# Moving seven of twelve modulation rows from TensorE, between attention units, to VectorE row sums

## The chip, the cores and the metric

The kernel runs on one core of one Trainium2 chip. The metric is the device time of one execution in microseconds (us). Five engines work side by side, each through a queue of its own in the order in which the program was built: TensorE (PE, with its weight loads as PEld), VectorE (DVE), ScalarE (ACT), GpSimd (POOL) and SyncE (SP), which issues the loads from memory. An instruction that waits holds up everything behind it on its engine.

## What is computed

Two transformer blocks follow each other. The first has two layers over 512 tokens (256 of a context, 256 of the sequence), and its normalised activations are shifted, scaled and gated by vectors that come from a condition:

```python
def adaln(cond, w_mod, b_mod):
    m = jnp.dot(jax.nn.silu(cond), w_mod) + b_mod
    return jnp.split(m[..., None, :], 6, axis=-1)

def modulate(h, shift, scale):
    return h * (1.0 + scale) + shift
```

`w_mod` is 1024 x 6144 for each layer, and there are two conditions (`c` for the sequence, `c_ctx` for the context), so a layer has six modulation rows ("which" 0 to 5: shift, scale and gate of the attention half, then of the feed-forward half) of 1024 numbers, for each condition. A layer is then: modulated norm, projections to q, k, v, a pooling branch and a convolution branch, four attention heads, an output projection gated by row 2, a modulated norm with rows 3 and 4, and a feed-forward of 1024 to 2816 to 1024 gated by row 5. In the second layer only the sequence's half of the tokens is carried past the keys and values, so that rows 2 to 5 are needed there for one condition. The second block (four branches, one layer) is untouched by the change.

## The kernel before

Activations lie with features on the 128 partitions and tokens along the free axis: `xT` is 128 x 8 x 512. Every large product is made of three fp32r products (high by high, low by high, high by low). `weights` (line 328) loads a 512 KB chunk of packed weights into `wraw` (4 buffers), ScalarE rounds it to `whi` (L333) and VectorE subtracts to get `wlo` (L334), each with 3 buffers; `mm3` (line 342) issues the three matmuls (L343 to L345). `feats` (line 359) makes one feature tile of 8 x 3 matmuls from one chunk, `tok` (line 387) makes token tiles.

`modulation` (line 491) is a generator that makes one group, one modulation row of one layer (1024 columns). In each of 8 steps a 512 KB chunk of `w_mod` comes into `wmod` (2 buffers), and four matmuls with 32 stationary columns (L497) add to the PSUM bank `ps_md`, of which there is one. After the eighth step ScalarE copies the bank (L502), TensorE transposes it twice (L504), and VectorE adds the bias (L517). Each of the four matmuls stands as two records in the trace, so that a step is 8 records.

`fill` (line 534) takes the next steps from `queue`, which holds groups 2 to 5 of layer 0 and all six of layer 1 (line 854). It is called at fixed places with the counts of `FILL` (line 28), n times four steps each: behind the transposes of each head's q and k (lines 893, 897 and 904), before the output projection (line 929), and behind the last product of the output projection and of the feed-forward (lines 941 and 984). The instructions get a lower priority than their neighbours. The order on each engine is then made by the Tile scheduler, which takes, of what is ready, the highest priority, and whose order is fixed when the program is built.

`attention` (line 636) goes over 16 units in layer 0 (4 heads x 4 token tiles) and 8 in layer 1. A unit's chain is: scores on TensorE, row maximum on VectorE (L651), exponential on ScalarE (L653), the weighted difference on VectorE (L662), transposes (L665), a copy on ScalarE (L667), the product with v (L670), the square on ScalarE (L674) and a scaled copy on VectorE (L675). `each` (line 875) runs after every unit. `project_rows` (line 818) makes the output projection in 16 steps of 12 matmuls (8 feature tiles in two parts), each closed by two VectorE additions into `xT` (L797). `norm` (line 467) makes the next `h` in two halves of 8 tiles (L479 on VectorE, or L476 and L477 on GpSimd, then L481 on ScalarE and L482 on VectorE). The feed-forward (from line 944) goes in three thirds of 8, 7 and 7 hidden tiles; a hidden tile is two `feats`, and a third ends with 8 projection steps.

Of the kernel before, what the change touches and what calls it, by code (L numbers as in the profile page):

```python
# [21 lines left out]
KD = D // 128  # L22
# [4 lines left out]

FILL = ((2, 2, 3, 3, 2, 1, 1), (2, 2, 2, 0, 0, 2, 9))
LATE = 60
AHEAD = (2, 0)  # L30
POOL_AFTER = ((14, 15), (5, 6))
# [5 lines left out]

MOD_GROUPS = {0: ((4, 5, 0, 1), (6, 7, 2, 3)) + tuple(tuple(range(4 * i, 4 * i + 4)) for i in (4, 2, 3, 5)),
              1: tuple(tuple(range(4 * i, 4 * i + 4)) for i in (1, 0, 4, 2, 3, 5))}

# [11 lines left out]
def _weight_plan():  # L52
# [3 lines left out]
    def rows(key, name, lead, cols, r0, kt):  # L56
        plan[key] = (name, lead, r0, np.asarray(cols), kt)

    qk_cols = (np.arange(8)[:, None] * 64 + HALVES[None, :]).ravel()
    for l in range(DEPTH):  # L60
        for g, parts in enumerate(MOD_GROUPS[l]):
            cols = np.concatenate([np.arange(c * 256, c * 256 + 256) for c in parts])
            for k in range(8):
                rows(("mod", l, g, k), "w_mod", (l,), cols, k * 128, 1)
        if l == 0:
# [51 lines left out]
def _pack_weights(inp):  # L117
    out = np.zeros((len(PLAN), 128, CHUNK), np.float32)
    for key, (name, lead, r0, cols, kt) in PLAN.items():
        a = np.asarray(inp[name])[lead]  # L120
        a = a[r0:r0 + kt * 128] if isinstance(r0, int) else np.concatenate([a[k * 128:k * 128 + 128] for k in r0])
# [49 lines left out]
def _rows():  # L171
    at, off = {}, 0
    for name, n in (("qkg", 256), ("subg", 256), ("qna", 64), ("kna", 64), ("qnc", 64), ("knc", 64), ("lnv", 512),
                    ("bf", 8)):
        at[name] = (off, n)
        off += n
    return at, off
# [5 lines left out]
def _pack_rows(inp):  # L183
    src = dict(qkg=np.stack([np.asarray(inp[n])[:, HALVES] for n in ("q_norm_g", "k_norm_g")]),
               subg=inp["subln_g"], qna=inp["qn_a_2"], kna=inp["kn_a_2"], qnc=inp["qn_c_2"],
               knc=inp["kn_c_2"], lnv=inp["ln_v_g_2"], bf=inp["b_forget_2"])
    return np.concatenate([np.asarray(src[k]).reshape(1, -1) for k in ROWS], axis=1)
# [78 lines left out]
def tile_two_blocks(ctx: ExitStack, tc: tile.TileContext, w: bass.AP, blk: bass.AP, cols: bass.AP,  # L266
# [30 lines left out]
    def open_consts(second):  # L297
        c0, c1 = (CST1, NCST) if second else (CST0, CST1)
        r0, r1 = (ROW1, NROWS) if second else (0, ROW1)
        ct = P["cst"].tile([128, c1 - c0], F32, name="cstt")  # L300
# [49 lines left out]
    def bank(p):  # L350
        return P[p].tile([128, 512], F32, name="ps_" + p)
# [181 lines left out]

    def fill(n, late=LATE):

        at = tc.cur_priority
        tc.cur_priority = at + late
        for _ in range(n * KD // 2):
            while queue and next(queue[0], None) is None:
                queue.pop(0)  # L540
        tc.cur_priority = at


# [303 lines left out]
    for l in range(DEPTH):  # L847
# [5 lines left out]
        if not last:  # L853
            queue.extend([modulation(0, g) for g in range(2, 6)] + [modulation(1, g) for g in range(6)])
        mix = {}
# [12 lines left out]
        def run_taps(m):  # L868
            for _ in range(min(m, len(taps))):
                taps.pop(0)()  # L870
# [4 lines left out]
        def each():  # L875
            run_taps(8)
            unit[0] += 1
            if jobs and unit[0] in POOL_AFTER[l]:
                jobs.pop(0)()
# [5 lines left out]
        for hd in range(0, 4, 2 if last else 1):  # L885
# [3 lines left out]
            if last:  # L889
                tok([("k", l, g, i) for i in range(2)], h, range(4),  # L890
                    lambda tt, p: rope(l, slice(1, 2), tt, kq[tt][:, 0:256], p))
                kT = to_feature(kq, 0, range(4))
                fill(FILL[l][hd])
                tok([("q", l, g, i) for i in range(2)], h, qts,
                    lambda tt, p: rope(l, slice(0, 1), tt, kq[tt][:, 256:512], p))
                qT = to_feature(kq, 256, qts)
                fill(FILL[l][hd + 1])
            else:
# [4 lines left out]
                kT = to_feature(kq, c + 128, range(4), 1)  # L903
                fill(FILL[l][hd])
            if hd == 0:
# [22 lines left out]
        conv_norm(l, acc, seqs, mix)  # L928
        fill(FILL[l][4])
        project_rows(l, range(KD), lambda d: merge(0, d), range(4), 2, False, 0, lo, None)  # L930
# [8 lines left out]
        project_rows(l, range(KD), lambda d: merge(1, d), range(4), 2, True, 0, lo, after)  # L939
        with tc.issue_after(P["product"].ins):  # L940
            fill(FILL[l][5], -50)

        for t, (f0, f1) in enumerate(THIRDS):
            hs = []
            f = f0
            items = []
            for f in range(f0, f1):
# [16 lines left out]
                for it in items:  # L964
                    feats([it], h, [(lo, 512)])
                items = []
            final = t == 2
            if final:
# [3 lines left out]
                def after2(d, a, b):  # L972
# [633 lines left out]
```

## Time and profile before

| what | value |
|---|---|
| time, median of 3 runs | 1467.88 us (1460.85, 1467.88, 1469.97) |
| the profiled execution's own time | 1452.94 us |
| its span in the trace | 1451.1 us |
| mean granted TensorE clock | 0.98 |
| busy PE, DVE, ACT, POOL | 1385.5, 854.4, 619.0, 233.3 us |

The span runs from the first to the last instruction of the profiled execution. Times below are microseconds from its start. A busy PE is pipelined matmuls, so that its busy time says when it had work, not how dense that was. In the span, the first norm ends at about 65, the attention of layer 0 runs from about 178 to 239, its output projection from 239 to 286.6, the norm behind it to 311, the three thirds of the first feed-forward from 311 to 655, the next norm and the start of layer 1 from 655, and the q, k and v of layer 1 to about 766.

### The profile page before, as it was taken

The page shows a single profiled execution, that of the slowest core. Times are in us where ns is not written, and L with a number is a line of the kernel's source. Part 1 is how long each engine was busy: PE and PEld are TensorE (multiplying, and loading weights), DVE is VectorE, ACT ScalarE, POOL GpSimd, SP SyncE. Part 2 cuts the span into 40 slices and gives each one's busy share as a digit, 9 for nine tenths or more (in the row PEclk, how much of TensorE's full clock was granted, in tenths as well). Part 3 has the DMA queues.
Part 4 walks back from the last instruction along what each step waited for, and adds up shares of the span by engine and source line. Part 5 has one row for each costly group of instructions (what it writes and reads, how often), then busy time and mean ns, then how long its engine had stood idle before and what let it go on. Part 6 is the DMA issues. An engine that isn't in the chain of part 4 may idle for free. (4 is left out here: it accounts for less than half of the span.)

```text
span 1451.1 us, 23265 instructions
## 1 busy us (share of the span) xinstructions
PE 1385.5 (95%) x9212; PEld 1191.6 (82%) x9212; DVE 854.4 (59%) x1592; ACT 619.0 (43%) x1100; POOL 233.3 (16%) x274
## 2 busy tenths in 40 slices
PE   5999999999999999999998899999989997999999
PEld 2787766888888888888867889999977887988999
DVE  4688665653333343338966655565786665657555
ACT  3333444342222222235344544444645549456443
POOL 0045440220000000013515210000452002000000
PEclk9999999999999999999999989999999999999999
DMA  8635654333322233225562335555743422434553
GB/s 332 238 117 195 204 196 146 103 115 102 97 91 102 86 104 102 90 85 189 198 227 71 106 127 187 176 189 174 240 148 113 148 77 78 146 113 149 189 178 128
DMA packets 60733, 212.49 MB, mean 146 GB/s; under 512 B 6864, under 2 KB 8016, under 8 KB 60368
## 3 DMA queue, kind: packets, MB, share of 16 engines
q1 hardware_dynamic: 60192, 208.85, 43.0%
q10 hardware_dynamic: 432, 2.16, 0.4%
q8 instruction: 72, 1.18, 0.3%
q14 instruction: 37, 0.30, 0.1%
HBM read 209.93 MB, written 1.05 MB: 145 GB/s over the span
## 5 line engine op out<-in xcount | busy, mean ns | idle before, releaser
L333 ACT CAST whi<-wraw 128x1024 fp32r<-128x1024 f32 (+2 forms) x296 | 304.8, 1033 | 536.2 <-PE ps_mm L344 268.8
L334 DVE TENSOR_TENSOR wlo<-wraw,whi 128x1024 fp32r<-128x1024 f32 (+2 forms) x296 | 359.6, 1217 | 229.1 <-ACT whi L333 225.7
L343 PE MATMUL ps_mm<-hH,whi 128*128 128x256 f32 (+1 forms) x1056 | 344.4, 328 | 7.7 <-ACT hH L481 7.0
L345 PE MATMUL ps_mm<-hH,wlo 128*128 128x256 f32 (+1 forms) x1056 | 342.7, 326 | 2.7 <-DVE wlo L334 2.7
L344 PE MATMUL ps_mm<-hL,whi 128*128 128x256 f32 (+1 forms) x1056 | 343.3, 326 | 0.3 <-DVE hL L482 0.3
L343 PEld LDWEIGHTS ps_mm<-hH,whi 128*128 128x128 f32 x1056 | 203.7, 194 | 29.0 <-ACT hH L481 9.3
L345 PEld LDWEIGHTS ps_mm<-hH,wlo 128*128 128x128 f32 x1056 | 204.4, 194 | 19.7 <-DVE wlo L334 3.3
L344 PEld LDWEIGHTS ps_mm<-hL,whi 128*128 128x128 f32 x1056 | 204.2, 194 | 19.6 <-issue 2.7
L343 PE MATMUL ps_mm<-hidH,whi 128*128 128x256 f32 (+1 forms) x683 | 214.9, 317 | 3.0 <-ACT hidH L339 1.7
L344 PE MATMUL ps_mm<-hidL,whi 128*128 128x256 f32 (+1 forms) x683 | 214.4, 315 | 0.6 <-DVE hidL L340 0.6
L345 PE MATMUL ps_mm<-hidH,wlo 128*128 128x256 f32 (+1 forms) x683 | 213.7, 314 | 0.0
L344 PE MATMUL ps_mm<-wlo,hH 128*128 128x256 f32 (+2 forms) x464 | 145.2, 314 | 3.3 <-DVE wlo L334 3.3
L343 PE MATMUL ps_mm<-whi,hH 128*128 128x256 f32 (+2 forms) x464 | 143.0, 317 | 0.6 <-ACT whi L333 0.6
L345 PE MATMUL ps_mm<-whi,hL 128*128 128x256 f32 (+2 forms) x464 | 143.2, 310 | 0.0
L343 PEld LDWEIGHTS ps_mm<-hidH,whi 128*128 128x128 f32 x683 | 129.2, 190 | 12.3 <-ACT hidH L339 1.9
L344 PEld LDWEIGHTS ps_mm<-hidL,whi 128*128 128x128 f32 x683 | 129.4, 189 | 9.2 <-DVE hidL L340 0.9
L345 PEld LDWEIGHTS ps_mm<-hidH,wlo 128*128 128x128 f32 x683 | 129.1, 190 | 8.1
L454 POOL TENSOR_TENSOR squares<-squares,scr 128x256 f32<-128x256 f32 (+1 forms) x28 | 30.2, 1077 | 562.3 <-ACT scr L453 561.9
L797 DVE SCALAR_TENSOR_TENSOR xT<-ps_mm,modv,xT 128x256 f32<-128x256 f32 x116 | 52.6, 479 | 99.0 <-PE ps_mm L345 98.8
L348 POOL TENSOR_TENSOR st<-st,mhalf 128x4 f32<-128x4 f32 (+3 forms) x54 | 67.3, 1251 | 214.7 <-DVE st L581 100.0
L344 PEld LDWEIGHTS ps_mm<-wlo,hH 128*128 128x128 f32 x464 | 88.5, 191 | 14.1 <-DVE wlo L334 6.1
L343 PEld LDWEIGHTS ps_mm<-whi,hH 128*128 128x128 f32 x464 | 87.3, 190 | 13.7 <-issue 8.3
(339 smaller groups left out, 1940.4 us busy)
## 6 DMA issues: line engine op xcount, KB each, us to landing
wraw<-in_w_dram SPq DMA_DIRECT2D x271, 512.0 KB, 3.5
wmod<-in_w_dram SPq DMA_DIRECT2D x85, 512.0 KB, 4.2
wraw<-in_w_dram SPq DMA_DIRECT2D x32, 448.0 KB, 3.2
xT<-in_x_dram ACTq DMA_DIRECT2D x2, 1024.0 KB, 6.9
single<-in_w_dram SPq DMA_DIRECT2D x8, 256.0 KB, 7.2
wraw<-in_w_dram SPq DMA_DIRECT2D x4, 288.0 KB, 2.8
out_dram<-scr SPq DMA_DIRECT2D x8, 128.0 KB, 1.7
tm<-in_blk_dram SPq DMA_DIRECT2D x3, 256.0 KB, 4.4
```

The lines of the kernel that those rows point to most:

```text
L333: act.copy(out=hi[:, :m], in_=t[:, :m])
L334: dve.tensor_tensor(lo[:, :m], t[:, :m], hi[:, :m].bitcast(F32), op=ALU.subtract)
L343: pe.matmul(ps, a[0], b[0], start=start, stop=False)
L344: pe.matmul(ps, a[0], b[1], start=False, stop=False)
L345: P["product"] = pe.matmul(ps, a[1], b[0], start=False, stop=stop)
L348: pool.tensor_tensor(t, t, mhalf[:, :n], op=ALU.pow)
L454: eng.tensor_tensor(squares[:, lo:hi], squares[:, lo:hi], q, op=ALU.add)
L797: dve.scalar_tensor_tensor(xT[:, d, r], ps[:, s * 256 - lo:s * 256 - lo + 256], M(l, which, 1 - s)[:, d:d + 1], xT[:, d, r], op0=ALU.mult, ...
```

## The change

Of the ten groups that went through `fill`, three stay (layer 0, rows 2, 4 and 3). They now run two steps after each of the first 12 attention units of layer 0. The other seven (layer 0 row 5, and all six of layer 1) are made by VectorE in a new generator, called three steps per hidden tile in the first feed-forward's code. For these `w_mod` is packed transposed, so that a chunk holds 128 output columns on the partitions and the 1024 inputs along the free axis; each half row of 512 is multiplied by the silu of the condition, spread over the partitions, and summed by one instruction into one column of `sums`. There are 8 chunks per row; a chunk takes 4 such sums where both conditions are needed (three rows) and 2 where one is (four rows). The product itself goes to the PSUM bank `ps_md` and is not read.

```diff
-FILL = ((2, 2, 3, 3, 2, 1, 1), (2, 2, 2, 0, 0, 2, 9))
+FILL = (2,) * 12
+BY_ROWS = ((0, 5), (1, 1), (1, 0), (1, 2), (1, 4), (1, 3), (1, 5))
+ROWS_PER_STEP = 3
...
+    def modulation_by_rows():
+
+        crow = [P["tm"].tile([128, 512], F32, name="tm") for _ in range(4)]
+        o = ROWS["cc"][0]
+        for i, t in enumerate(crow):
+            dma.dma_start(out=t, in_=rowv[:, o + i * 512:o + i * 512 + 512].broadcast_to([128, 512]))
+            act.activation(t, t, AF.Silu)
+        for l, which in BY_ROWS:
+            js = range(2 if l == 0 or which < 2 else 1)
+            sums = {j: st(16) for j in js}
+            for d in range(KD):
+                t = raw_chunk(("modr", l, which, d), "wmod")[0]
+                for j in js:
+                    for i in range(2):
+                        dve.tensor_tensor_reduce(bank("md"), t[:, i * 512:i * 512 + 512], crow[2 * j + i], 1.0, 0.0,
+                                                 ALU.mult, ALU.add, sums[j][:, i * KD + d:i * KD + d + 1])
+                if d < KD - 1:
+                    yield
...
-            queue.extend([modulation(0, g) for g in range(2, 6)] + [modulation(1, g) for g in range(6)])
+            queue.extend(modulation(0, g) for g in range(2, 5))
...
         def each():
             run_taps(8)
+            if not last and unit[0] < len(FILL):
+                fill(FILL[unit[0]])
...
-                fill(FILL[l][hd])
...
-        fill(FILL[l][4])
...
-        with tc.issue_after(P["product"].ins):
-            fill(FILL[l][5], -50)
-
+        rows = modulation_by_rows() if not last else None
...
+                if not last:
+                    for _ in range(ROWS_PER_STEP):
+                        next(rows, None)
...
-        with tc.issue_after(P["product"].ins):
-            fill(FILL[l][6], -50)
```

Where the seven rows land is decided by the scheduler. The first place is VectorE's queue in the output projection of layer 0 (`xT` is the addition that closes a step, `wlo` the low half of a weight chunk, `hidL` the low half of an attention output). Before:

```order
L797 SCALAR_TENSOR_TENSOR xT<-ps_mm,modv_112,xT 128x256 x4
L334 TENSOR_TENSOR wlo<-wraw,whi 128x1024
L340 TENSOR_TENSOR hidL<-ps_aux,hidH 128x512
L340 TENSOR_TENSOR hidL<-cacc,hidH 128x512 x2
L797 SCALAR_TENSOR_TENSOR xT<-ps_mm,modv_112,xT 128x256 x4
L334 TENSOR_TENSOR wlo<-wraw,whi 128x1024
L797 SCALAR_TENSOR_TENSOR xT<-ps_mm,modv_112,xT 128x256 x4
```

And in the changed kernel, where `ISA ps_md` is a sum and `ISA st` the read of its accumulator:

```order
L567 ISA ps_md,st_3321<-wmod,tm 128x512
L567 ISA st_3321 128x1
L835 SCALAR_TENSOR_TENSOR xT<-ps_mm,modv_112,xT 128x256 x2
L567 ISA ps_md,st_3320<-wmod,tm 128x512
L567 ISA st_3320 128x1
L344 TENSOR_TENSOR wlo<-wraw,whi 128x1024
L835 SCALAR_TENSOR_TENSOR xT<-ps_mm,modv_112,xT 128x256 x2
L567 ISA ps_md,st_3320<-wmod,tm 128x512
L567 ISA st_3320 128x1
L835 SCALAR_TENSOR_TENSOR xT<-ps_mm,modv_112,xT 128x256 x2
```

The sums have moved up: counted over the whole queue, 64 of the 160 stand ahead of the first norm behind the attention (from the tenth unit on), 19 inside that norm, and 77 in the first third of the feed-forward; none stands behind it.

The second place is ScalarE's queue in the attention of layer 0, where `e` is the exponential and `tm` at L559 the silu of the spread condition. In the changed kernel:

```order
L559 ACT_TABLE_LOAD
L559 ACTIVATE tm<-tm 128x512
L712 ACTIVATE sq_1720,st_1674<-ps_aux,st_1707 128x128
L705 COPY aT<-ps_aux 128x256
L559 ACTIVATE tm<-tm 128x512
L691 ACT_TABLE_LOAD
L691 ACTIVATE e,st_1906<-ps_sc,st_1905 128x256
L559 ACT_TABLE_LOAD
L559 ACTIVATE tm<-tm 128x512
L691 ACT_TABLE_LOAD
L691 ACTIVATE e,st_1906<-ps_sc,st_1905 128x256
L559 ACT_TABLE_LOAD
```

In the kernel before there is one table load ahead of the first exponential of that attention and none between its units. A piece of its queue there, with the same square, copy and exponential:

```order
L674 ACTIVATE sq_1940,st_1894<-ps_aux,st_1927 128x128
L667 COPY aT<-ps_aux 128x256
L653 ACTIVATE e,st_2070<-ps_sc,st_2069 128x256
L674 ACTIVATE sq_1980,st_1894<-ps_aux,st_1967 128x128
L653 ACTIVATE e,st_2070<-ps_sc,st_2069 128x256
L667 COPY aT<-ps_aux 128x512
```

So four silus and six table loads now stand between the exponentials, three changes to the silu table and three back.

The third place is TensorE's queue at the start of layer 1, where `tm` is transposed for keys and queries. Before:

```order
L497 MATMUL ps_md<-wmod,csil 32x256
L620 MATMUL ps_aux<-first,tm 128x128 x2
L497 MATMUL ps_md<-wmod,csil 32x256 x3
L343 MATMUL ps_mm<-whi,hH 128x256
L344 MATMUL ps_mm<-wlo,hH 128x256
L345 MATMUL ps_mm<-whi,hL 128x256
```

And in the changed kernel:

```order
L658 MATMUL ps_aux<-first,tm 128x128 x2
L355 MATMUL ps_mm<-whi,hL 128x256
L353 MATMUL ps_mm<-whi,hH 128x256
L354 MATMUL ps_mm<-wlo,hH 128x256
L355 MATMUL ps_mm<-whi,hL 128x256
L353 MATMUL ps_mm<-whi,hH 128x256
```

The modulation's matmuls are gone there, and the projections stand directly behind the transposes.

## Rows read from the trace of the kernel before

**Rows 1.** The page's first part: busy time, share and instructions by engine

```profile
PE 1385.5 (95%) x9212; PEld 1191.6 (82%) x9212; DVE 854.4 (59%) x1592; ACT 619.0 (43%) x1100; POOL 233.3 (16%) x274
```

**Rows 2.** Stretches: start:end, length, busy by engine (instructions), clock, DMA share, GB/s

```profile
core 0: us, PE busy (x) PEld busy (x) DVE busy (x) ACT busy (x) POOL busy (x), PEclk, DMA share, GB/s
65.00:178.00 113.00, 113.00 (x885) 91.74 (x885) 90.40 (x171) 41.99 (x101) 49.69 (x55) 1.00 0.50 169
178.00:202.80 24.80, 23.68 (x164) 15.45 (x161) 17.41 (x38) 11.31 (x34) 16.60 (x31) 1.00 0.62 213
202.80:239.00 36.20, 31.93 (x236) 19.73 (x236) 22.75 (x60) 19.23 (x54) 6.43 (x8) 0.95 0.62 203
239.00:286.60 47.60, 47.60 (x261) 41.25 (x259) 27.17 (x53) 16.41 (x26) 8.97 (x8) 1.00 0.21 69
286.60:311.00 24.40, 21.36 (x175) 19.20 (x174) 15.97 (x33) 10.64 (x23) 10.65 (x11) 0.93 0.37 127
311.00:446.00 135.00, 135.00 (x605) 112.09 (x605) 51.34 (x61) 37.63 (x46) 0.00 (x0) 1.00 0.31 102
655.00:690.00 35.00, 33.67 (x251) 28.17 (x251) 29.22 (x63) 18.45 (x33) 12.54 (x11) 0.90 0.56 196
690.00:766.00 76.00, 74.17 (x625) 58.79 (x623) 57.94 (x125) 31.85 (x73) 31.44 (x32) 1.00 0.61 208
```

**Rows 3.** The same stretches, the modulation's matmuls (L497) alone: PE, PEld, clock, DMA

```profile
65.00:178.00 113.00, 20.37 (x182) 5.51 (x182) 1.00 0.50 169
202.80:239.00 36.20, 8.31 (x104) 2.04 (x104) 0.95 0.62 203
286.60:311.00 24.40, 2.38 (x32) 0.77 (x32) 0.93 0.37 127
655.00:690.00 35.00, 5.71 (x52) 1.57 (x52) 0.90 0.56 196
690.00:766.00 76.00, 14.43 (x172) 4.00 (x172) 1.00 0.61 208
```

**Rows 4.** Groups by line: the modulation's matmuls and transposes; busy, mean ns, idle before

```profile
L497 PE MATMUL ps_md<-wmod,csil 128*32 128x256 f32 x640 | 59.7, 393 | 9.8 <-DMA wmod<-in_w_dram 9.7
...
L504 PE MATMUL ps_md<-first,cp 128*128 128x128 f32 x20 | 4.2, 295 | 0.0
```

**Rows 5.** Groups by line and form: VectorE instructions over 512 elements; busy, mean ns

```profile
L340 DVE TENSOR_TENSOR hidL<-scr,hidH 128x512 fp32r<-128x512 f32 x24 | 16.3, 684 | 0.0
L662 DVE SCALAR_TENSOR_TENSOR e<-e,st 128x512 f32<-128x512 f32 x16 | 13.4, 839 | 0.5
```

**Rows 6.** Timeline of VectorE: multiply-and-reduce of the second block; start, length

```profile
1281.08 0.42 DVE L1346 CUSTOM_DVE_ANT_0 e<-ps_sc,cstt 128x256 f32<-128x256 f32 x1
...
1281.43 0.29 DVE L1346 CUSTOM_DVE_ANT_0 e<-ps_sc,cstt 128x128 f32<-128x128 f32 x1
...
1281.64 0.42 DVE L1346 CUSTOM_DVE_ANT_0 e<-ps_sc,cstt 128x256 f32<-128x256 f32 x1
```

**Rows 7.** Groups by line: ScalarE's table load, and an activation over 512 elements

```profile
L653 ACT ACT_TABLE_LOAD x2 | 2.6, 1283 | 0.0
...
L952 ACT ACTIVATE scr<-ps_mm 128x512 f32<-128x512 f32 x21 | 12.4, 589 | 0.0
```

**Rows 8.** Timeline of VectorE in the first feed-forward: two weight chunks

```profile
330.33 1.23 DVE L334 TENSOR_TENSOR wlo<-wraw,whi 128x1024 fp32r<-128x1024 f32 x1
...
335.76 1.22 DVE L334 TENSOR_TENSOR wlo<-wraw,whi 128x1024 fp32r<-128x1024 f32 x1 [3.61 <-ACT whi L333]
```

**Rows 9.** Loads of wmod: from issue to landing

```profile
DMA to landing us min/median/max: 3.3/4.2/10.3
```

**Rows 10.** Timelines of VectorE and GpSimd: pairs of convolution taps, one beside GpSimd

```profile
82.20 1.40 DVE L769 SCALAR_TENSOR_TENSOR cacc<-cu,colt,cacc 128x512 f32<-128x512 f32 x2
...
87.78 1.87 DVE L769 SCALAR_TENSOR_TENSOR cacc<-cu,colt,cacc 128x512 f32<-128x512 f32 x2
...
87.92 1.19 POOL L607 TENSOR_TENSOR tm<-tm,own 128x256 f32<-128x256 f32 x1
```

More of the change, by code (lines that the diff above doesn't have):

```diff
@@ L34 @@
 NXS = 3
-MOD_GROUPS = {0: ((4, 5, 0, 1), (6, 7, 2, 3)) + tuple(tuple(range(4 * i, 4 * i + 4)) for i in (4, 2, 3, 5)),
-              1: tuple(tuple(range(4 * i, 4 * i + 4)) for i in (1, 0, 4, 2, 3, 5))}
+MOD_GROUPS = {0: ((4, 5, 0, 1), (6, 7, 2, 3)) + tuple(tuple(range(4 * i, 4 * i + 4)) for i in (2, 4, 3))}
 MIX_PARTS = ((0, 1, 4, 5), (6, 7, 2, 3))
@@ L60, in _weight_plan @@
     for l in range(DEPTH):
-        for g, parts in enumerate(MOD_GROUPS[l]):
+        for g, parts in enumerate(MOD_GROUPS.get(l, ())):
             cols = np.concatenate([np.arange(c * 256, c * 256 + 256) for c in parts])
@@ L64, in _weight_plan @@
                 rows(("mod", l, g, k), "w_mod", (l,), cols, k * 128, 1)
+        for which in range(6):
+            if (l, which) in BY_ROWS:
+                for d in range(8):
+                    plan[("modr", l, which, d)] = ("w_mod", (l,), ("T", which * D + d * 128), np.arange(D), 1)
         if l == 0:
@@ L120, in _pack_weights @@
         a = np.asarray(inp[name])[lead]
+        if not isinstance(r0, int) and r0[0] == "T":
+            out[INDEX[key]] = a[:, r0[1]:r0[1] + 128].T
+            continue
         a = a[r0:r0 + kt * 128] if isinstance(r0, int) else np.concatenate([a[k * 128:k * 128 + 128] for k in r0])
@@ L173, in _rows @@
     for name, n in (("qkg", 256), ("subg", 256), ("qna", 64), ("kna", 64), ("qnc", 64), ("knc", 64), ("lnv", 512),
-                    ("bf", 8)):
+                    ("bf", 8), ("cc", 2048)):
         at[name] = (off, n)
@@ L185, in _pack_rows @@
                subg=inp["subln_g"], qna=inp["qn_a_2"], kna=inp["kn_a_2"], qnc=inp["qn_c_2"],
-               knc=inp["kn_c_2"], lnv=inp["ln_v_g_2"], bf=inp["b_forget_2"])
+               knc=inp["kn_c_2"], lnv=inp["ln_v_g_2"], bf=inp["b_forget_2"],
+               cc=np.stack([np.asarray(inp["c"])[0], np.asarray(inp["c_ctx"])]))
     return np.concatenate([np.asarray(src[k]).reshape(1, -1) for k in ROWS], axis=1)
@@ L298, in open_consts @@
         c0, c1 = (CST1, NCST) if second else (CST0, CST1)
-        r0, r1 = (ROW1, NROWS) if second else (0, ROW1)
+        r0, r1 = (ROW1, ROWS["cc"][0]) if second else (0, ROW1)
         ct = P["cst"].tile([128, c1 - c0], F32, name="cstt")
@@ L532, in tile_two_blocks, with fill @@
     queue = []
-    def fill(n, late=LATE):
+    def fill(n):
         at = tc.cur_priority
-        tc.cur_priority = at + late
-        for _ in range(n * KD // 2):
+        tc.cur_priority = at + LATE
+        for _ in range(n):
             while queue and next(queue[0], None) is None:
@@ L541, in fill @@
         tc.cur_priority = at
+    def modulation_by_rows():
[15 more added lines that the diff above has]
+                    yield
+            bias = C(f"bmod{l}")[:, which * 8:which * 8 + 8]
+            for j in js:
+                m = M(l, which, j)
+                dve.tensor_tensor(m, sums[j][:, :KD], bias, op=ALU.add)
+                dve.tensor_tensor(m, m, sums[j][:, KD:], op=ALU.add)
+                if which in (1, 4):
+                    g, to = ("n1g", scale1) if which == 1 else ("n2g", scale2)
+                    dve.scalar_tensor_tensor(to[l][:, j], m, 1.0, C(g)[:, l * 8:l * 8 + 8], op0=ALU.add, op1=ALU.mult)
+            yield
     coef = {}
@@ L896, in tile_two_blocks @@
                 qT = to_feature(kq, 256, qts)
-                fill(FILL[l][hd + 1])
             else:
@@ L903, in tile_two_blocks @@
                 kT = to_feature(kq, c + 128, range(4), 1)
-                fill(FILL[l][hd])
             if hd == 0:
```

## The prediction

> **What bounds the kernel now.** I read the page's first part, then a table of stretches, the modulation's own instructions in the same stretches, its groups by line, VectorE's groups over 512 elements, three timelines, and the landing of the modulation's loads.
>
> The first part shows TensorE busy for 1385.5 us, 95% of the span, with VectorE at 59% [rows 1]. On that alone, work moved from TensorE to VectorE is a gain. The modulation's matmuls keep TensorE busy for 59.7 us in 640 records, 0.746 us for a step of 8, and TensorE waits 9.8 us for them, nearly all of it for loads of `wmod` [rows 4]. Seven groups of ten go: 56 steps (41.8 us), 7 pairs of transposes at 4.2 / 10 = 0.42 us, and at most the whole wait: 54.5 us is the most that can be gained.
>
> The stretches show that VectorE's 59% is a mean over unlike places [rows 2]. In 65 to 202.8 it is busy for 107.8 of 137.8 us; from 202.8 to 311 for 65.9 of 108.2; in the first third of the feed-forward for 51.3 of 135; at the start of layer 1 for 87.2 of 111. The clock was 0.90 or more everywhere, so it prices nothing here. The order puts 64 of the 160 sums in 202.8 to 286.6, 19 in 286.6 to 311 and 77 in 311 to 446. So the question is what a sum costs, and whether VectorE has that room where the sums stand, not where they were written.
>
> **The price of a sum.** No row shows it. The nearest of its kind is the second block's multiply-and-reduce, which also reads an accumulator: from the start of the 256-wide one to the next 0.35 us, from the 128-wide one to the next 0.21 [rows 6]. On that line 512 elements cost 0.35 + 256 x 0.14 / 128 = 0.63; I take 0.615 as the lower end, since these read PSUM and a sum reads SBUF only. Plain instructions with two operands over 512 elements take 0.684 and, from `st`-scaled `e`, 0.839 [rows 5]. That is the upper side. I take 0.70, by the nearer row, 0.684, and a little for the accumulator.
>
> **The change, stretch by stretch.** Sums are made against the profiled execution's own 1452.94 us (a span of 1451.1 and 1.84 around it). It lies 15 us under the median; I add the difference to the median.
>
> *65 to 202.8.* There are 24 steps after the change, two behind each of 12 units, with their 24 loads of 512 KB. Before there were 20.37 us (182 records, 23 steps) to 178 [rows 3] and 11 steps more to 202.8, so 10 steps and a pair go: -7.9 us. VectorE at 90.4 of 113 is almost a second bound there, so that not all of this comes back. Against it stand four silus at 0.589 and six table loads at 1.283 [rows 7], 10.1 us on ScalarE, between exponentials of about the eighth and ninth unit. Behind each of them on ScalarE stand the exponential, the copy and the rounding of weights, for which VectorE and TensorE wait. ScalarE is busy for only 11.3 of 24.8 us there [rows 2], so that between nothing and all 10.1 is hidden. I take +6, and **-2** for the stretch (-8 to +2). The four loads of the spread condition (256 KB each) come before it, among the DMA's 0.5 to 0.62 share, and cost nothing that I can name.
>
> *202.8 to 286.6, the end of the attention and the output projection.* TensorE loses 8.31 us and 6 more of its 4.27 idle (36.20 - 31.93) with transposes [rows 2, 3]; it was the bound. VectorE had 22.75 + 27.17 = 49.9 us of 83.8 and gets 64 x 0.70 = 44.8: 94.7, which is 10.9 more than the stretch lasted. Each closing addition into `xT` has sums ahead of it on VectorE; behind those wait `wlo` and then the next step's matmuls. With some 3 us of VectorE's own waits left I take **+14** (+5.5 at 0.615 with 0.2 us of waits; +22 at 0.80 with 5). There is a gain here only if a sum costs under 33.9 / 64 = 0.53 us. The wait for `wmod` does not vanish either: it moves to VectorE, where a sum whose chunk has not landed holds the additions. 16 chunks in 84 us leave 5.2 us for each, and two buffers need (2.8 + 4.2) / 2 = 3.5, so I cost it at nothing.
>
> *286.6 to 311, the norm.* TensorE had 21.36 us of 24.40 and loses 2.38 and up to 3.04 of idle. VectorE had 15.97 and gets 19 x 0.70 = 13.3: 29.3, or +4.9 [rows 2, 3]. GpSimd and ScalarE do part of the norm and can run ahead, so I take **+4** (0 to +9).
>
> *311 to 446, the first third.* VectorE goes from 51.3 to 51.3 + 53.9 = 105 of 135 us: it fits. The new user is memory. A hidden tile's `feats` takes 335.76 - 330.33 = 5.43 us with one 512 KB chunk [rows 8], about 97 GB/s, which agrees with the stretch's 102 [rows 2]; three `modr` chunks per two `feats` come on top, hoisted as early as buffers allow. Where a chunk has two sums, two buffers give a cycle of 1.4 us of sums and 4.2 us of landing (3.3 to 10.3) [rows 9]: 5.6 us, against 5.43. `wlo` has three buffers, so a late VectorE is felt only after about two `feats`, 10.9 us. I take **+2** (0 to +13).
>
> *446 to 655* has no sum and no step: nothing.
>
> *655 to 766, the start of layer 1.* TensorE loses 5.71 + 14.43 = 20.1 us [rows 3], four pairs of transposes (1.7) and about 1.8 us of the wait for `wmod`: 23.6. Where it alone was the bound that would all come back. But VectorE is busy for 29.22 + 57.94 = 87.2 of 111 us [rows 2], so that 111 - 23.6 = 87.4 leaves it no gap at all; each `tm` transposed needs its rows from VectorE first. I take **-15** (-24 to -8).
>
> Small edits, at nothing: 7 copies of the bank on ScalarE go; 23 additions over 8 columns replace as many over 8 and 16; the row 5 that gates the feed-forward is due 135 us after its last sum.
>
> The sum is -2 + 14 + 4 + 2 - 15 = **+3**, so 1456 on this execution and 1467.88 + 3 = 1471 on the median.
>
> **A rule weighed.** Rows first: a pair of taps over 512 elements on VectorE takes 1.40 us alone and 1.87 beside a GpSimd instruction of 1.19 us [rows 10], 0.47 lost, or 0.4 us for each us of GpSimd. The Trainium skill ("SBUF — State Buffer", section "Who interferes with whom") says that a VectorE instruction with two inputs in SBUF contends with a GpSimd instruction that reads SBUF; a sum has two such inputs. By that, GpSimd's 6.43 + 8.97 + 10.65 = 26 us in 202.8 to 311, of which sums would meet about 83 x 0.70 / 108 = 0.54, would cost 26 x 0.54 x 0.4, about 5.6 us more: an estimate that makes the total about +9. The row agrees with the rule, but shows it for the taps, and I leave the sum at +3.
>
> **The rivals.**
> 1. *VectorE has the room after all* (faster). A sum at 0.615, ScalarE's detour hidden under TensorE's steps, and layer 1 giving back 20 of its 23.6: -7 + 5.5 + 0 + 0 - 20 = -21.5, so 1446. For it speaks the multiply-and-reduce [rows 6]; against it VectorE's 87.2 us in layer 1.
> 2. *A sum is dear* (slower). Sums at 0.84, the price of the other three-operand instruction [rows 5], beside GpSimd or because each waits for the one before, which writes the same bank. The output projection and the attention's end go to 49.9 + 53.8 - 83.8 + 3 = +22.9, the norm to +7.5: with -2, +2 and -15 that is +15.4, about 1483. It is over 1% from a price of about 0.83.
> 3. *The first feed-forward starves* (slower). With two loads and the weights on the same queues a `modr` chunk lands in 5.5 us; the cycle is 6.9 against 5.43, and over 16 chunks that is 23 us, less the 10.9 that `wlo`'s buffers cover: +12.5 for +2, so the sum is +13.5, and with 5.6 us of landing over +15: 1483. It decides from a landing of about 5.5 us. For it speaks the maximum of 10.3 [rows 9], against it a mean of 102 GB/s where 213 were moved elsewhere [rows 2].
>
> That the change does not do what it says is half true by the order already: more than half of the sums do not stand in the feed-forward. It is in the forecast.
>
> **How the numbers follow.** About 1% (14.7 us) is what a measurement of this kernel can tell from no change. The forecast, no change that can be told, gets 0.45: the gains of two stretches and the losses of two are alike in size and rest on one unknown price. Rival 1 gets 0.25, rival 2 0.17, rival 3 0.13; so faster 0.25, same 0.45, slower 0.30. The bounds added up give -26.5 to +46, which is too wide for 8 in 10, since they would not all fall on one side. The range reaches past rival 1 and to both slower rivals with some of each other's price: 1444 to 1495. The forecast's own range is 1457 to 1483.
>
> **What would show it.** In the changed kernel: the sums' mean with the accumulator's read (0.70; over 0.83 rival 2, near 0.6 rival 1); VectorE nearly without idle time between the last units and the norm, with that stretch at some 98 us for 83.8; six table loads among the units' exponentials with VectorE's maximum and TensorE waiting behind them; about 192 records of the modulation's matmuls and the next stretch to the norm's end 4 us longer; 311 to 446 unchanged, with the landing of `wmod` near 4 us; layer 1's 111 us at about 96, with VectorE as the releaser of TensorE's waits. I am wrong in the mechanism if the output projection does not lengthen though the sums stand in it, or if layer 1 does not shorten; in size if a sum costs outside 0.6 to 0.84.

## The result and the profile after

The changed kernel takes 1457.14 us (median of 9 runs, 1451.95 to 1463.0) against 1466.25 us for the kernel before (9 runs, 1460.85 to 1469.97): a ratio of 0.9939, 95% interval 0.9918 to 0.9961. It is 0.6% faster, clear of noise and under the 1% that the prediction drew its line at. The time lies in the predicted range; the forecast of +3 us has the wrong sign.

The profiled execution of the changed kernel took 1457.94 us, near its median. The one of the kernel before that stands ahead of the prediction took 1452.94 us, 13 us under its own. So the two traces differ by +5.0 us while the medians differ by -9.1. That contradiction is the subject of most of what follows.

The page's first part for the changed kernel, which answers to [rows 1]:

```profile
PE 1367.4 (94%) x8750; PEld 1195.1 (82%) x8750; DVE 959.2 (66%) x1924; ACT 623.2 (43%) x1100; POOL 233.3 (16%) x274
```

TensorE has 462 instructions fewer, but only 18.1 us less busy time, and its mean granted clock is 0.957 where that profile of before had 0.98. VectorE has 104.8 us more.

Stretches of the changed kernel, cut at the same instructions as those of before (last exponential of the first attention, last addition into `xT`, end of the norm, last addition of the feed-forward); they answer to [rows 2]:

```profile
core 0: us, PE busy (x) PEld busy (x) DVE busy (x) ACT busy (x) POOL busy (x), PEclk, DMA share, GB/s
52.00:235.00 183.00, 171.46 (x1142) 136.34 (x1141) 144.78 (x305) 85.72 (x198) 72.12 (x92) 0.91 0.40 136
235.00:295.80 60.80, 54.13 (x267) 44.72 (x266) 59.83 (x151) 19.35 (x31) 9.58 (x8) 0.93 0.43 144
295.80:323.00 27.20, 22.14 (x148) 21.42 (x149) 27.17 (x72) 9.16 (x21) 12.08 (x12) 0.81 0.30 105
323.00:673.90 350.90, 347.46 (x1595) 288.87 (x1593) 184.25 (x334) 97.30 (x120) 7.67 (x7) 1.00 0.45 149
```

From 235 to 323 VectorE is busy for 87.0 of 88.0 us, as the prediction had it. TensorE is busy for 76.3 of them, at a clock of 0.93 and 0.81. The same two stretches took 53.3 and 20.4 us in the profile of before, at 0.97 and 0.92. The feed-forward's 350.9 us are 350.2 there.

The sums: first all of them as one group (the 21.8 us at its end are VectorE's idle time ahead of sums, 19.9 of it for loads of `wmod`), then on VectorE's timeline in the output projection:

```profile
L567 DVE CUSTOM_DVE_ANT_0 ps_md<-wmod,tm 128x512 f32<-128x512 f32 x160 | 114.7, 717 | 21.8 <-DMA wmod<-in_w_dram 19.9
```

```profile
242.00 0.88 DVE L835 SCALAR_TENSOR_TENSOR xT<-ps_mm,modv,xT 128x256 f32<-128x256 f32 x2
242.80 0.69 DVE L567 CUSTOM_DVE_ANT_0 ps_md<-wmod,tm 128x512 f32<-128x512 f32 x1
243.40 0.14 DVE L567 DVE_READ_ACCUMULATOR2_ANT st<- 128x1 f32 x1
243.58 0.70 DVE L567 CUSTOM_DVE_ANT_0 ps_md<-wmod,tm 128x512 f32<-128x512 f32 x1
244.20 0.14 DVE L567 DVE_READ_ACCUMULATOR2_ANT st<- 128x1 f32 x1
244.37 0.70 DVE L567 CUSTOM_DVE_ANT_0 ps_md<-wmod,tm 128x512 f32<-128x512 f32 x1
244.99 0.14 DVE L567 DVE_READ_ACCUMULATOR2_ANT st<- 128x1 f32 x1
245.21 0.88 DVE L835 SCALAR_TENSOR_TENSOR xT<-ps_mm,modv,xT 128x256 f32<-128x256 f32 x2
```

From one sum to the next behind it are 243.58 - 242.80 = 0.78 and 0.79 us: 0.70 for the sum, then the accumulator's read, which overlaps with its end, and a gap. Between two pairs of additions into `xT`, three sums take 2.4 us. The idle time ahead of sums harms little: 21.2 us of it lie in the first third of the feed-forward, which takes 122.6 us for 120.4 before, and 0.5 in the output projection.

ScalarE's timeline in the first attention shows one of the three detours to the silu's table and back:

```profile
188.86 1.28 ACT L691 ACT_TABLE_LOAD   x1
190.16 0.47 ACT L691 ACTIVATE e<-ps_sc,st 128x256 f32<-128x256 f32 x1
190.53 0.19 ACT L691 ACTIVATION_READ_ACCUMULATOR e<-ps_sc,st 128x1 f32 x1
190.74 1.28 ACT L559 ACT_TABLE_LOAD   x1
192.03 0.63 ACT L559 ACTIVATE tm<-tm 128x512 f32<-128x512 f32 x1
192.68 1.28 ACT L691 ACT_TABLE_LOAD   x1
193.98 0.47 ACT L691 ACTIVATE e<-ps_sc,st 128x256 f32<-128x256 f32 x1
```

Between one exponential and the next, ScalarE spends 0.63 us on a silu and 2.56 us on tables.

### The profile page after: what moved, and what is told of

Read it like the earlier page. It is cut to its first block, busy times and chain, and to the rows that moved or that the text cites. A ratio compares the mean times of both kernels' runs of the same rounds, so it can differ in the third digit from the quotient of the medians.

```text
span 1455.8 us, 22714 instructions
## 1 busy us (share of the span) xinstructions
PE 1367.4 (94%) x8750; PEld 1195.1 (82%) x8750; DVE 959.2 (66%) x1924; ACT 623.2 (43%) x1100; POOL 233.3 (16%) x274
## 5 line engine op out<-in xcount | busy, mean ns | idle before, releaser
L567 DVE CUSTOM_DVE_ANT_0 ps_md<-wmod,tm 128x512 f32<-128x512 f32 x160 | 114.7, 717 | 21.8 <-DMA wmod<-in_w_dram 19.9
```

Of the source, the lines that this page charges most:

```text
L567: dve.tensor_tensor_reduce(bank("md"), t[:, i * 512:i * 512 + 512], crow[2 * j + i], 1.0, 0.0, ALU.mult, ALU.add, sums[j][:, i * KD + d:i ...
```

## The experiments

Two questions were open: where the contradiction between traces and medians comes from (theory 1, TensorE's clock, against theory 2, the work), and what each part of the change costs (theory A, VectorE's queue ahead of the feed-forward, against theory B, work only moved).

### The kernel before, again

Nothing is edited. With these three the kernel before has four profiles.

> The kernel before, unchanged, for the clocks of its ordinary executions. The profiled execution shown ahead of the prediction took 1452.94 us at a mean granted clock of 0.98, less than each of its nine timed runs (1460.85 to 1469.97). Theory 1, the clock: ordinary executions have a clock of 0.96 to 0.97 and a median near 1466, and a profile of one of them shows full-speed stretches of the shown profile at less than 1.0; then the sum of the prediction was made against an execution that ordinary ones do not resemble. Theory 2, the work: the clock is 0.98 again and the 13 us lie in waits elsewhere. Ratio to the kernel before: 1.000 by both.

> The kernel before, unchanged, profiled as the last of a series. Theory 1, the clock: its profile has a mean clock of 0.960 to 0.972 and a time of 1462 to 1474 us, and the time above the 1452.94 us of the profile shown first lies in stretches whose granted clock is lower than there. Theory 2: at such a time the clock of each stretch is as in the profile shown first.

> The kernel before, unchanged, for a fourth profile. Theory 1: the same stretch takes 82 to 88 us at an execution time of 1459 us or more, with a clock of 0.9 or less in it. Rival: anything from 75 to 86, without regard to the time of the execution.

The three profiled executions took 1459.23 us at a clock of 0.975, 1467.15 at 0.968 and 1465.32 at 0.971. Over the 68 executions of this kernel that came with these experiments the time falls as the clock rises, from 1477.9 us at 0.957 to 1458.78 at 0.974 and 1459.49 at 0.975, with a correlation of -0.95, and the 1452.94 us at 0.980 shown ahead of the prediction lie beyond the far end of that row, where its straight line gives 1454.5. Theory 1 holds for this kernel. The stretch where it shows best is that of the second layer's second pair of heads and its output projection, here in the profile shown ahead of the prediction and in the second of the three later ones (1467.15 us):

```profile
753.50:798.30 44.80, 38.62 (x267) 31.04 (x266) 28.95 (x64) 22.19 (x59) 26.25 (x38) 0.92 0.26 89
798.30:831.20 32.90, 30.29 (x242) 29.03 (x240) 23.51 (x47) 17.26 (x33) 7.68 (x9) 1.00 0.31 97
```

```profile
756.80:805.80 49.00, 43.46 (x264) 34.19 (x263) 28.94 (x64) 22.39 (x59) 26.94 (x38) 0.79 0.24 81
805.80:842.70 36.90, 34.69 (x244) 33.01 (x242) 22.78 (x47) 17.30 (x33) 7.23 (x8) 0.86 0.27 86
```

VectorE's, ScalarE's and GpSimd's work is the same to 0.8 us. TensorE's clock is 0.79 and 0.86 instead of 0.92 and 1.00, and the stretch takes 85.9 us instead of 77.7. Pieces of it, in the shown profile and then in the later one:

```profile
776.00:781.00 5.00, 3.05 (x18) 1.60 (x16) 4.10 (x8) 2.51 (x6) 3.98 (x10) 1.00 0.62 212
781.00:786.00 5.00, 3.94 (x11) 2.79 (x11) 1.36 (x4) 1.97 (x5) 0.93 (x2) 0.55 0.10 40
786.00:791.00 5.00, 5.00 (x24) 4.15 (x25) 2.39 (x5) 1.30 (x3) 0.00 (x0) 0.77 0.00 0
791.00:796.00 5.00, 4.63 (x24) 2.98 (x23) 4.52 (x7) 3.76 (x11) 3.22 (x4) 1.00 0.32 107
```

```profile
788.00:793.00 5.00, 5.00 (x16) 3.36 (x14) 1.73 (x4) 0.78 (x2) 0.00 (x0) 0.50 0.00 0
793.00:798.00 5.00, 5.00 (x18) 3.63 (x17) 1.72 (x3) 1.99 (x4) 0.64 (x1) 0.50 0.00 0
798.00:803.00 5.00, 5.00 (x17) 3.35 (x17) 3.02 (x5) 2.50 (x7) 4.64 (x5) 0.50 0.33 108
803.00:808.00 5.00, 3.92 (x17) 3.27 (x16) 3.80 (x10) 2.40 (x7) 0.73 (x1) 0.50 0.00 0
```

In the later profile the clock is at 0.50 for 20 us, that is 1.2 of 2.4 GHz, with TensorE busy for 18.9 of them. In the shown one it falls at the same place, behind 5 us in which TensorE was busy for only 3.05, but it is back at 1.00 within 10 us.

### The changed kernel, again

> The changed kernel, unchanged, for a second profile. The stretch from the end of the second layer's first attention half to the last addition of its output projection has the same instructions in both kernels; it took 77.7, 83.9 and 85.9 us in three profiles of the kernel before and 75.8 in the one of the changed kernel. Theory 1, its length differs between the kernels in ordinary executions through TensorE's clock: 74 to 79 us here. Rival: it varies from execution to execution alike in both: anything from 75 to 86.

> The changed kernel, unchanged, for a third profile. Theory 1: the same stretch takes 74 to 79 us. Rival: anything from 75 to 86.

They took 1457.74 us at 0.958 and 1460.34 at 0.954. That stretch took 75.8 us, as in the first profile, and then 82.2. So theory 1 holds for the kernel before and only half for the changed one: the length varies in both. The three later profiles of before have 83.9 to 85.9; of the changed kernel two have 75.8 and one 82.2. The last one in its two parts:

```profile
757.40:802.40 45.00, 39.45 (x228) 32.87 (x229) 28.12 (x63) 21.66 (x58) 26.98 (x38) 0.81 0.15 48
802.40:839.60 37.20, 34.95 (x244) 33.06 (x243) 22.75 (x46) 17.39 (x34) 7.28 (x8) 0.86 0.26 86
```

Again the low clock, 0.81 and 0.86, goes with the long stretch.

That the stretch has the same instructions in both kernels, as was expected, is not so at its start: four modulation steps of the kernel before stand there, to 766 in the shown profile. Up to the first exponential of its units the kernel before takes 27.2 to 27.5 us and the changed one 28.7, so that nothing is gained there. From that exponential on the work is the same (304 and 303 matmuls, no modulation step in either). That part took 50.2 us in the shown profile, 56.7, 58.6 and 56.7 in the later ones, and 47.1, 47.1 and 53.6 in the changed kernel.

### Sums and silus behind the norm

```diff
+        P["ndve_ffn"], P["nact_ffn"] = P["ndve"], P["nact"]
...
-                    for _ in range(ROWS_PER_STEP):
-                        next(rows, None)
+                    with tc.issue_after(P["ndve_ffn"].ins), tc.issue_after(P["nact_ffn"].ins):
+                        for _ in range(ROWS_PER_STEP):
+                            next(rows, None)
```

`ndve` and `nact` are the norm's last instructions on VectorE and ScalarE.

> The changed kernel with all 160 sums and the four silus held behind the last instruction of the norm ahead of the first feed-forward, on VectorE and ScalarE; nothing else changes. Theory A, VectorE's queue: the sums cost 14 us in the output projection and the norm and the silus some us in the attention, and the feed-forward takes them at nothing: 16 to 25 us under the changed kernel, ratio to the kernel before 0.976 to 0.984. Theory B, the work is only moved: 112 us of sums in the feed-forward hold up the low halves of the weights there; within 5 us of the changed kernel, ratio 0.990 to 0.997.

1437.15 us, ratio 0.9782 (0.9745 to 0.9819): 20 us under the changed kernel by the medians and 23 by the ratios, as theory A had it, sums and silus together. The norm ends at 292.4 instead of 323.0, 30.6 us earlier, and of these the feed-forward gives back 7.8: its second third takes 122.0 us, against 112.7 in the changed kernel. The three thirds:

```profile
292.40:413.60 121.20, 121.20 (x555) 101.04 (x554) 114.78 (x274) 35.05 (x43) 0.00 (x0) 1.00 0.66 212
413.60:535.60 122.00, 116.09 (x501) 94.65 (x500) 81.85 (x179) 29.38 (x36) 0.00 (x0) 0.99 0.67 212
535.60:651.10 115.50, 115.46 (x573) 98.02 (x572) 42.14 (x54) 33.63 (x44) 7.67 (x7) 1.00 0.28 92
```

A piece of VectorE's timeline at 442 to 446:

```profile
442.08 0.70 DVE L567 CUSTOM_DVE_ANT_0 ps_md<-wmod,tm 128x512 f32<-128x512 f32 x1 [0.51 <-DMA wmod<-in_w_dram]
...
443.49 1.22 DVE L344 TENSOR_TENSOR wlo<-wraw,whi 128x1024 fp32r<-128x1024 f32 x1
446.05 0.70 DVE L567 CUSTOM_DVE_ANT_0 ps_md<-wmod,tm 128x512 f32<-128x512 f32 x1 [1.34 <-DMA wmod<-in_w_dram]
```

Crowded sums wait for their loads there, 23.3 us in the second third, with the low halves of the weights behind them on VectorE: in small, the prediction's third rival.

### Without the seven rows

```diff
-                        dve.tensor_tensor_reduce(bank("md"), t[:, i * 512:i * 512 + 512], crow[2 * j + i], 1.0, 0.0,
-                                                 ALU.mult, ALU.add, sums[j][:, i * KD + d:i * KD + d + 1])
...
+                dve.tensor_copy(m, bias)
```

> The changed kernel without the 160 sums, their 56 loads and the silus: the seven modulation rows are the bias alone, so that part of the computation is left out. What is left is the whole gain of taking 56 steps off TensorE. Theory A: within 4 us of the kernel with the sums behind the norm, about 0.975 to 0.982 of the kernel before, because sums in the feed-forward cost nothing. Theory B: 10 us or more below that kernel. If it is above 0.985, TensorE's steps were never worth their 41.8 us, since VectorE or the clock takes their place.

1430.81 us, ratio 0.9731 (0.9699 to 0.9763). This is the floor: the 56 steps, with their transposes and waits, are worth some 39 us, where the prediction had 54.5 at most. It is 6 us under the kernel with the sums behind the norm, between both theories' numbers, which that kernel's second third explains: 122.0 us, against 114.3 without rows.

### A copy for the silu

```diff
-            act.activation(t, t, AF.Silu)
+            act.copy(out=t, in_=t)
```

> The changed kernel with a copy in place of each of the four silus, so that the silu of the condition is left out of the seven rows; the six table loads among the exponentials go, and every engine's order else is the same. Theory A: the detour of 10.1 us on ScalarE is on the path by about 6: 4 to 8 us under the changed kernel. Rival: the sums on VectorE hide it, 0 to 2 us under the changed kernel.

1449.94 us, ratio 0.9875 (0.984 to 0.991), 0.64% under the changed kernel's 0.9939, or some 9 us; by the medians 7. Stretches to the end of the norm:

```profile
51.20:226.30 175.10, 165.41 (x1143) 132.60 (x1141) 144.79 (x306) 77.80 (x192) 72.23 (x92) 0.95 0.41 142
226.30:287.40 61.10, 54.22 (x267) 44.93 (x266) 59.93 (x151) 19.44 (x32) 9.62 (x8) 0.92 0.43 144
287.40:314.60 27.20, 22.80 (x148) 21.69 (x149) 27.18 (x71) 9.13 (x21) 12.39 (x12) 0.76 0.30 104
```

The first stretch takes 175.1 us instead of 183.0: 7.9 less, and ScalarE is busy for 7.9 less in it. The six table loads are 7.7 us; the four copies take as long as the silus did. So the table changes were on the path in full. The two stretches behind, full of sums, stay as long as they were.

### Silus behind the attention

```diff
-                    for _ in range(ROWS_PER_STEP):
-                        next(rows, None)
+                    with tc.issue_after(P["exp"].ins):
+                        for _ in range(ROWS_PER_STEP):
+                            next(rows, None)
```

`P["exp"]` is the last exponential of the attention. It holds back the silus, and the sums wait for these.

> The changed kernel with the four silus held behind the last exponential of the first layer's attention, where one table load serves them and the feed-forward's own silus; the sums, which need them, stand in the output projection, the norm and the first feed-forward. Theory A, VectorE's queue is full wherever sums stand ahead of the norm: the projection and the norm get over 60 sums at 0.79 us from start to start and lengthen by 20 to 28 us against the kernel with the sums behind the norm; 1452 to 1460 us, ratio 0.988 to 0.994. Rival: the detour of the silus was what the changed kernel lost, and the sums hide; 1437 to 1443 us, ratio 0.978 to 0.983.

1447.1 us, ratio 0.9875 (0.9855 to 0.9896): between the two ranges that were expected. From the last exponential to the end of the norm:

```profile
221.50:283.00 61.50, 54.96 (x270) 45.67 (x270) 59.12 (x149) 21.61 (x36) 10.23 (x8) 0.92 0.42 139
283.00:309.90 26.90, 22.16 (x148) 20.77 (x149) 26.55 (x66) 9.04 (x21) 11.37 (x12) 0.81 0.34 115
```

VectorE is busy for 85.7 of 88.4 us, and the two are together that long, against 72.0 us in the kernel with the sums behind the norm: +16.4, somewhat less than the 20 to 28 expected, and 10 us in the median. The feed-forward, with fewer sums to crowd it, takes 352.5 us, 6.2 less than there. The mechanism of theory A holds, its size was high.

### Sums spread over the feed-forward

On top of the kernel with the sums behind the norm:

```diff
-                    with tc.issue_after(P["ndve_ffn"].ins), tc.issue_after(P["nact_ffn"].ins):
-                        for _ in range(ROWS_PER_STEP):
+                    with tc.issue_after(P["split"].ins), tc.issue_after(P["nact_ffn"].ins):
+                        for _ in range(2 if f <= 12 else 4):
                             next(rows, None)
```

`P["split"]` is the last VectorE instruction of the hidden tile just made.

> The kernel with the sums behind the norm, but spread: each hidden tile's sums are held behind that tile's last VectorE instruction, two chunks for each of the first twelve tiles and four for each of the rest, so that they go through all three thirds. Theory A, VectorE and the loads were crowded in the second third (122.0 us against 114.3 without sums): it returns to 114 to 117 and the kernel takes 1430 to 1434 us, ratio 0.973 to 0.977. Rival: memory traffic of 56 loads of 512 KB beside the weights costs the same wherever they stand in the feed-forward; 1436 to 1440 us, ratio 0.978 to 0.981.

1428.91 us, ratio 0.9749 (0.9725 to 0.9774): faster than the kernel before and the changed one, by 2.5% and about 1.9%. Its ratio cannot be told from that of the kernel that makes no rows at all. The three thirds:

```profile
292.70:412.90 120.20, 120.20 (x551) 100.39 (x551) 85.51 (x173) 34.91 (x44) 0.00 (x0) 1.00 0.49 162
412.90:527.10 114.20, 114.20 (x505) 94.55 (x505) 82.07 (x176) 29.81 (x36) 0.00 (x0) 1.00 0.56 180
527.10:646.70 119.60, 117.43 (x574) 99.16 (x572) 76.81 (x158) 33.81 (x44) 7.67 (x7) 0.99 0.57 185
```

The second third has its 114 us back with 82 us of VectorE work in it, as much as when it took 122.0; the third now pays 4 us. All three take 354.0 us, for 358.7 with the sums crowded and 350.0 without rows. So the sums and their loads cost nothing in the first two thirds, at two chunks for a hidden tile, and 4 us in the last one, at four.

### What the removed steps were worth in layer 1

```diff
+                pe.matmul(ps[g * 32:g * 32 + 32, :256], csil[:, k % KD, :], csil.rearrange("p k j -> p (k j)"),
+                          start=True, stop=True, tile_position=(0, g * 32))
...
+                filler(10)
...
+                filler(6)
```

The ten steps stand behind the transposes of k, the six behind those of q.

> The evenly spread kernel with 32 steps of four matmuls whose result is not used, put into the second layer's q, k and v (10 behind the transposes of k and 6 behind those of q, for each pair of heads), where the kernel before had its modulation steps; they read a constant and wait for no load. At 0.746 us a step that is 23.9 us more on TensorE. Theory C, the clock: the steps of the kernel before stood partly in TensorE's waits and kept its clock at 1.00 there, where the evenly spread kernel has 0.89 (672.7 to 733.1); the filler brings the stretch back to 0.97 or more and costs little: 1426 to 1436 us, ratio 0.973 to 0.980. Theory D, only the work counts: most of 23.9 us is paid, 1442 us or more, ratio 0.984 or more.

1440.22 us, ratio 0.982 (0.9788 to 0.9852), between the two. From the feed-forward's last addition to the end of the first pair of heads, in the kernel before, the changed one, and the one with the filler:

```profile
658.00:753.50 95.50, 93.92 (x748) 75.46 (x742) 77.72 (x162) 42.89 (x85) 35.39 (x31) 0.96 0.61 213
```

```profile
673.90:761.40 87.50, 78.09 (x552) 72.63 (x552) 76.91 (x156) 42.06 (x82) 32.19 (x31) 0.88 0.30 97
```

```profile
647.40:739.80 92.40, 90.57 (x806) 74.69 (x801) 77.74 (x157) 41.87 (x82) 28.72 (x31) 1.00 0.30 92
```

The steps were 17.2 us of TensorE's time there. Without them it is busy for 15.8 us less, its clock is 0.88, and 8.0 us come off. The filler is 18.8 us by the trace (23.9 were expected). With it the clock is at 1.00, and the stretch is 6.0 us longer than in the evenly spread kernel (646.7 to 733.1, 86.4 us at 0.90): of the 18.8 us, 7.9 stand where TensorE was idle there, and the other matmuls keep it busy for 4.9 us less at the higher clock. So a third to a half of the steps' time comes back when they go. Theory C is right about the clock, and theory D about there being a price; most of the rest of the median's 11 us lies in the attention behind it, 44.4 us at a clock of 0.85 for 40.1 at 0.96.

```diff
+            if last:
+                filler(2)
```

> The evenly spread kernel with two such unused steps behind each of the eight attention units of the second layer, 16 steps or 11.9 us of TensorE at 0.746 us. In the profile of the kernel before that stood near its median, the clock was 0.50 from about 788 to 808 there; in the evenly spread kernel the same stretch had 0.96. Theory C: the filler stands in waits for ScalarE and VectorE and the clock stays at or above 0.96: within 4 us of the evenly spread kernel, ratio 0.973 to 0.978. Theory D: the 11.9 us are paid, ratio 0.982 to 0.984.

1441.23 us, ratio 0.9811 (0.9771 to 0.9852). The scheduler moved all 16 steps ahead of the units, to 650 to 709, so that this run does not answer what it asked. The stretch ahead of the units grew by 3.5 us to 89.9, and the attention and projection behind took 81.6 us, against 74.1 in the evenly spread kernel, at a clock of 0.85 and 0.86. Its executions run from 1431.33 us at a clock of 0.970 to 1446.25 at 0.956, once more along the clock.

## Why the prediction was wrong

The stretches of the trace, by length in us, rounded. "Ordinary" is the mean of the three later profiles of the kernel before; the changed kernel has three profiles too, and the next column is their mean.

| stretch | forecast | before, shown | before, ordinary | changed, first | changed, mean | change on shown | change on ordinary |
|---|---|---|---|---|---|---|---|
| to the end of the first norm | 0 | 51.2 | 51.5 | 52.0 | 51.8 | +0.8 | +0.4 |
| attention and output projection of layer 0 | +12 | 236.2 | 237.4 | 243.8 | 242.5 | +7.6 | +5.2 |
| norm | +4 | 20.4 | 22.4 | 27.2 | 27.2 | +6.8 | +4.7 |
| first feed-forward | +2 | 350.2 | 350.2 | 350.9 | 351.7 | +0.7 | +1.4 |
| start of layer 1 | -15 | 95.5 | 94.3 | 87.5 | 86.9 | -8.0 | -7.5 |
| its attention and output projection | 0 | 77.7 | 84.7 | 75.8 | 77.9 | -1.9 | -6.8 |
| all the rest | 0 | 619.9 | 621.6 | 618.6 | 618.6 | -1.3 | -3.0 |
| sum | +3 | 1451.1 | 1462.1 | 1455.8 | 1456.6 | +4.7 | -5.5 |

**The step that failed** is the one from the execution to the median: "It lies 15 us under the median; I add the difference to the median", with "The clock was 0.90 or more everywhere, so it prices nothing here" ahead of it. Against the shown execution the sum came out right to 2 us, in part by luck: the attention was 4.4 us too high and layer 1 7.0 us too hopeful. But that execution's clock of 0.980 was one that the kernel before rarely has: of those 68 none is above 0.975. The 15 us were no constant to be carried over to the changed kernel, but time at a low clock, most of it where the two kernels' work is the same: 7.1 of the 11.0 us between shown and ordinary lie in the second layer's second half of the attention and its projection, behind the last modulation step. That part, which the prediction put at nothing, takes 57.3 us in the ordinary profiles of before and 49.2 in the changed kernel, -8.1; everything else together is +2.5, close to the forecast. The changed kernel's median stands where its own profile stands, so the difference came out as -9 instead of +3. Nor did the clock price nothing in the changed kernel: it is 0.88 at the start of layer 1 and 0.81 in the norm. The table ahead of the prediction gave the warning: a profiled time below all three timed runs.

**What stays open.** The change on ordinary profiles is -5.5 us, where the medians say -9.1. The profiles fell that way: the three of before took 2.4 us less than their kernel's median on the average, the three of the changed kernel 1.5 more. But why the changed kernel spends less time at the low clock in that part is not shown. In the five other kernels without steps or filler in layer 1 it took 47.0 to 53.8 us, so that all eight such profiles lie below the 56.7 to 58.6 of the three ordinary ones of before (the shown one, with 50.2, lies among them). Steps just ahead of it are the obvious reason, but with filler in their place it took 50.9 and 50.7, within the changed kernel's own spread, and a filler inside the units could not be placed.

**The price of a sum** was forecast at 0.70 us and is 0.79 from start to start: 0.70 is what the sum alone takes, and the accumulator's read was left out of it in effect. For 64 + 19 sums that is +7.5 us on the two stretches ahead of the feed-forward. The attention and projection still came out below the forecast. With a copy for the silu they took 236.2 us, as in the shown profile, so that sums and steps cancel there, where the forecast had -8 and +14. Without rows they took 220.3, so that the steps were worth 15.9. That their worth was set too low is the likely reason.

**The silus**' detour was forecast at +6 of 10.1 us. Its table changes alone cost 7.9.

**The saturated VectorE** was right, in place and in kind: 1.0 us of idle time from 235 to 323, additions into `xT` behind sums, and most of the cost gone when the sums are held back. **The first feed-forward** was right at +2 in its first third (+2.2), of which the second gave 1.6 back. The cycle of two buffers showed as 21.2 us of VectorE's waits, which TensorE felt little of; with all 160 sums there it felt more.

**Layer 1** was right in kind and half in size, -8 for -15. Of TensorE's idle time, 1.6 us before and 9.4 after, only 1.2 us end with VectorE; 4.1 end with exponentials, which wait for row maxima, and 3.3 with GpSimd's squares in the norm. So the reason given, that VectorE would be left no gap, is not what shows (it is busy for 76.9 of 87.5 us). The steps had stood largely in TensorE's waits, and as they went the clock fell to 0.88, which costs some 2.5 us: an estimate from 78.1 us of busy time after, and 75.6 before without the steps and their transposes.

**The rule on GpSimd** was estimated at 5.6 us. A sum beside GpSimd's squares took 1.73 us, one just ahead of them 0.68. By the Trainium skill ("SBUF — State Buffer", section "Who interferes with whom") a VectorE instruction with two inputs in SBUF contends with a GpSimd instruction that reads SBUF, and the trace agrees with it here. VectorE's timeline, and GpSimd's at the same time:

```profile
286.03 0.68 DVE L567 CUSTOM_DVE_ANT_0 ps_md<-wmod,tm 128x512 f32<-128x512 f32 x1
...
287.03 1.73 DVE L567 CUSTOM_DVE_ANT_0 ps_md<-wmod,tm 128x512 f32<-128x512 f32 x1
```

```profile
286.91 2.43 POOL L464 TENSOR_TENSOR squares<-squares,scr 128x512 f32<-128x512 f32 x2 [3.29 <-ACT scr L463]
```

But only 17 of 160 sums overlap with a GpSimd instruction by more than 0.3 us, with a mean of 0.89 us against 0.70 for the others: 3.2 us in all.

**Slips of the working.** The bounds add up to +38, not +46. Of the 56 steps 11, not 10, leave the stretch to 202.8: [rows 3] have 45 of them behind it. The sentence on TensorE's loss in the output projection cannot stand as it is, since 6 us are not part of 4.27; 8.31 us of matmuls and up to 4.27 of waits is what the rows allow. And the sums of the first third come two chunks to a `feats`, not three to two. None of these turns the sign.

The rivals: the first (faster by 21.5 us) had the direction, with the wrong reason, since no sum was cheap and no table change hidden. The second and third had their mechanisms, small.

## What to carry to other kernels

Before a sum is made against one profiled execution, see whether that execution is like the timed ones; where its time is below all of them and its clock above, compare the kernels at ordinary clocks, or the sum's sign can be the profile's and not the change's. Work moved to an engine "with room" has to be held where that room is: here the same sums and silus cost some 28 us more when left to the scheduler ahead of a full stretch than when they were tied, evenly, to the hidden tiles of the feed-forward, where the time could not be told from that without them. An activation that needs another table belongs where that table is loaded anyway.

## What was not expected of the hardware

The same program took from 1458.78 to 1477.9 us as its mean granted clock went from 0.974 to 0.957, about 1.0 us for each thousandth (the slope over the 68 executions); an attention stretch of some 80 us took 77.7 at a clock of 0.92 and 1.00 in its two parts, and 85.9 at 0.79 and 0.86. And matmuls that compute nothing, 18.8 us of them, lengthened a stretch by only 6.0 us: 7.9 us of them stood in TensorE's idle time, and the clock rose from 0.90 to 1.00, with the other matmuls 4.9 us shorter.
